# Gate products as one 512-column and one 256-column matmul, and more vector time per product for the RWKV chain, in a hybrid gated layer on one core

## Chip, cores and metric

One core of one Trainium2 chip. The metric is the device time of one execution in microseconds. Engines are named as the profile names them: PE (TensorE matmul), PEld (its weight loads), DVE (VectorE), ACT (ScalarE), POOL (GpSimd, which also issues the chain's DMAs), SP (SyncE, which issues the weight loads). Line numbers are those of the kernel before; the changed kernel's are one higher.

## What is computed

One layer for 256 tokens of width 2048. A normed input is projected to four gate sections (2048 columns each) and to four mixers of width 512: a gated linear recurrence (branch a), forgetting attention ("Fox", branch b), an SSD branch (c) and an RWKV-7 branch (d). The part that the change touches is

```
gates = sigmoid(xn @ w_gate).reshape(B, S, 4, D)
merged = sum over j of gates[:, :, j] * (branch_j @ w_branch[j])
h = h + merged @ w_out
```

and the RWKV-7 branch, a recurrence over tokens with a 64x64 state in each of 8 heads. A gated feed-forward (`w_up`, a 3-tap convolution, `w_down`) and a second gated input follow.

## The kernel before

**Products in three parts.** Activations lie transposed, in 16 row blocks of 128 by 256 tokens. A value is split into a high part and a remainder, and a product is hi·hi + hi·lo + lo·hi. Weights come from DRAM in chunks of 512 KB (`chunk`, L205, four buffers `wr`). ACT makes the high part `wh` (L214) and VectorE the remainder `wl` (L215), in three buffers each. An activation block `x` holds its high part in columns 0 to 255 and its remainder in columns 256 to 511.

`gemm_fm` takes four chunks to a block of two 128-row halves. Given such an `x`, it calls `product`: `wh` against all 512 columns of `x`, `wl` against the first 256. The result has two parts, and `joined` brings them together (an ACT copy, L256, and a VectorE addition). Given a pair of tiles, it issues three matmuls of 256 columns into one 256-column result. The gates take the pair form (`xg`, the halves of `xs`), and their evacuation is one VectorE multiplication by the row scale `R` straight from PSUM, then a tanh on ACT. All of these matmuls have the line L132 and write tiles `pg`.

**Order of the work.** After the projections come 32 gate blocks, eight to a branch, in the order a, c, b (Fox), d (RWKV). In the first three branches each gate block is followed by a branch block (`branch_unit`: 24 matmuls with the split branch output, from tiles `sb`). The gates of d are done alone, and its branch blocks at the end. Before the first block of a branch, `ready` splits the branch's four output tiles into eight tiles of the pool `bp` (36 buffers), which the RWKV chain uses too.

**The RWKV chain.** It is a generator, launched after the last projection. `hook` calls `pump` after each half of each chunk. A pump adds RATE to a credit, of at most three times RATE. If the credit is positive, it lets the generator run to its next `yield` and subtracts the vector time that the step recorded, a fixed STEP, and RATE times the number that the `yield` hands over (a pause in pumps). The chain's instructions have a lower priority than the gates' on every engine but TensorE, where they are put 16 places behind the current product. A list scheduler in the build sets the final order of each engine from these priorities and from what is ready by its own time.

The chain has these parts: token shift; per-head quantities for four blocks j, which end in masked 64x64 products (tiles `beb`, `kab`) and go to DRAM as `rw_j`; a loop of 31 steps on VectorE that inverts 32x32 triangles (a product and a reduction, L930); a copy of the inverse on ACT (L935); two writes to DRAM (`rw_q`, L937 and L938); six loads of it back as blocks (`qbd`, L945, and `qat`, L941); two blocks of small matmuls, first `qat` x `ltb`, copied to `xt1` by L952, then `qbd` x `xt1`; four steps over 64 tokens each, c = 0 to 3, with transposes (copies L1002), products with `qbd`, and a state update; and a per-head normalization. Its matmuls have the line L135 and write tiles `pb`. Only after all this can the branch blocks of d begin.

Of the kernel before, what the change touches and what calls it, by code (L numbers as in the profile page):

```python
# [11 lines left out]
ALU = mybir.AluOpType  # L12
# [3 lines left out]
S = 256  # L16
# [3 lines left out]

DELAY, RATE, STEP = 16, 0.5, 0.2
D_FF = 5632
NF = D_FF // P
IN_COLS = 14092
# [59 lines left out]
def body(tc, T, out, dbg=None):  # L86
# [5 lines left out]
    def shape_n(ap):  # L92
        n = 1
        for s in ap.shape[1:]:
            n *= s
        return n

    def tt(o, a, b, op):
        cost[0] += 0.07 + shape_n(o) / 960.0
        V.tensor_tensor(o, a, b, op=op)  # L100

    def mul(o, a, b):
        tt(o, a, b, ALU.mult)

    def add(o, a, b):
        tt(o, a, b, ALU.add)
# [19 lines left out]
    def act(o, i, f, **kw):  # L126
        A.activation(o, i, f, **kw)  # L127
# [10 lines left out]
    def mm(o, l, r, start=True, stop=True):  # L138
        on_pe(PE.matmul, o, l, r, start=start, stop=stop)
# [11 lines left out]
    def lane(name):  # L151
        prio[cur[0]] = tc.cur_priority
        cur[0] = name
        tc.cur_priority = prio[name]
# [13 lines left out]
    def slot(dt=F32, pool=sp):  # L168
        return pool.tile([P, S], dt, name="sb" if pool is not sp else "s", tag="s")

    def bank():
        return psB.tile([P, 512], F32, name="pb", tag="pb")
# [9 lines left out]
    def bslot(dt=F32):  # L182
        return slot(dt, bp)
# [19 lines left out]
    def chunk(src, kn, cols, eng=None):  # L203
        wr = wp.tile([P, kn, cols], F32, name="wr", tag="wr", bufs=4)
        (eng or dma_w).dma_start(wr, src)  # L205
        return wr
# [3 lines left out]
    def split(wr, kn, cols):  # L210

        wh = wp.tile([P, kn, cols], F32R, name="wh", tag="wh", bufs=3)
        wl = wp.tile([P, kn, cols], F32R, name="wl", tag="wl", bufs=3)
        A.copy(wh, wr)  # L214
        V.tensor_tensor(wl, wr, wh.bitcast(F32), op=ALU.subtract)  # L215
        newest[0] = wl
        return [(wh[:, i], wl[:, i]) for i in range(kn)]
# [21 lines left out]
    def halves(x):  # L239
        return (x[:, :S], x[:, S:]) if not isinstance(x, tuple) else x  # L240

    def product(pt, xs, k, nk, ms, w, fresh=True):


        wh, wl = w
        x = xs[k]
        if k == 0:
            mm(pt, wh[:, ms], x, start=fresh, stop=False)
            mm(pt[:, :S], wl[:, ms], x[:, :S], start=False, stop=False)
        else:  # L250
            mm(pt[:, :S], wl[:, ms], x[:, :S], start=False, stop=False)
            mm(pt, wh[:, ms], x, start=False, stop=k == nk - 1)

    def joined(o, pt):

        A.copy(o, pt[:, S:])  # L256
        add(o, o, pt[:, :S])

    def gemm_fm(W, xs, evac, each=None):

        ncol = S if each is None else 2 * S
        nm, nk = ncol // P, KD if each else len(xs)
        pts = [(gbank if m < 2 else bank)() for m in range(nm)]
        step = 1024 // ncol
        k0 = 0
        if each is not None:
            lane("m")
            for i in range(3):  # L270
                mm(pts[0], warm[:, :P], warm, start=i == 0, stop=False)
        while k0 < nk:
            kn = min(step, nk - k0)
            lane("g")
            if each is not None:
                kn = 1 if k0 < 4 else 2
            if each is None:
                w = chunk(W[k0 // step].rearrange("p (k n) -> p k n", k=kn), kn, ncol)
            else:
                w = chunk(W[k0:k0 + kn].rearrange("k p n -> p k n"), kn, ncol)  # L280
                each(k0, kn)
            w = split(w, kn, ncol)
            lane("m")
            for m in range(nm):
                ms = slice(m * P, m * P + P)
                for k in range(kn):
                    if not isinstance(xs[k0 + k], tuple):
                        product(pts[m], xs, k0 + k, nk, ms, w[k], not (each and m == 0))
                        continue
                    xh, xl = xs[k0 + k]  # L290
                    wh, wl = w[k]
                    first, last = k0 + k == 0, k0 + k == nk - 1
                    pt = pts[m][:, :S]
                    mm(pt, wh[:, ms], xh, start=first, stop=False)
                    mm(pt, wh[:, ms], xl, start=False, stop=False)
                    mm(pt, wl[:, ms], xh, start=False, stop=last)
                if hook[0]:
                    hook[0]()
            k0 += kn
        lane("g")  # L300
        if each is not None:
            each(nk, 0)
        for m in range(nm):
            evac(m, pts[m])
        lane("b")
# [25 lines left out]
    def mm2(o, l, src, start=True, stop=True, pool=sp):  # L331

        h, lo = split_act(src, pool=pool)
        mm(o, l, h, start=start, stop=False)
        mm(o, l, lo, start=False, stop=stop)
# [34 lines left out]
    xraw, xs = [], []  # L370
# [19 lines left out]
    R = cst.tile([P, S], F32, name="R")  # L390
# [415 lines left out]
    def rwkv():  # L806
# [3 lines left out]
        u = raw["du"]  # L810
# [10 lines left out]
        pt = bank()  # L821
        for j in range(4):
            s = bslot()
# [119 lines left out]
        for hb in range(4):  # L943
            bs = slice(hb * 32, hb * 32 + 32)
            dq.dma_start(qbd[bs, :, (hb % 2) * 32:(hb % 2) * 32 + 32],  # L945
                         bass.AP(tensor=q_d.tensor, offset=q_d.offset + hb * 16 * 1024, ap=blk))
        yield 9
        px = bank()
        for i in range(16):
            for h in (1, 0):  # L950
# [14 lines left out]
        for c in range(4):  # L965
# [27 lines left out]
            for k in (3, 2, 1, 0):  # L993
                if k not in tk and k + 1 not in tk:
                    continue
                pt = bank()
# [34 lines left out]
        for j in range(4):  # L1031
            pt = bank()
            mm2(pt[:, :S], center, yT[:, j], pool=bp)
            o = bslot()
            A.copy(o, pt[:, :S])
            yc.append(o)
            yield
        for j in range(4):
            s = bslot()
            act(s, yc[j], AF.Square)  # L1040
            mm2(pr[:8, :S], selR[:, j], s, j == 0, j == 3, bp)
            yield
        w = [bslot() for _ in range(3)]
        rstd_of(w[0][:8], pr[:8, :S], 64.0, 64e-5, w[1][:8], w[2][:8])
        nbc = head_bcast(bcast_rows(w[0][:8], 8, "rw_gn"))
# [41 lines left out]

    active = []

    credit = [0.0]  # L1090

    def pump():

        credit[0] = min(credit[0] + RATE, 3 * RATE)
        if not active or credit[0] <= 0:
            return
        was = cur[0]
        lane("b")
        cost[0] = STEP
        g = active[0]  # L1100
        try:
            credit[0] -= RATE * (next(g) or 0)
        except StopIteration:
            active.remove(g)
        credit[0] -= cost[0]
        lane(was)
# [7 lines left out]
    def proj(name, u0, n):  # L1114
        raw[name] = []
        for u in range(n):
            gemm_fm(T["w_p"][u0 + u], xs, evac_raw(raw[name]))
# [3 lines left out]
    def launch(name, f):  # L1121
        gens[name] = f()
        active.append(gens[name])
# [28 lines left out]
    launch("b", fox)  # L1152
    proj("du", 12, 7)
    launch("d", rwkv)


    merged = [None] * KD
# [1 line left out]
    order = [(0, "a"), (2, "c"), (1, "b"), (3, "d")]  # L1159
    gates = {}  # L1160

    xg = [halves(x) for x in xs]

    def gate_unit(j, u, pool):
        def ev_g(m, pt):
            s = slot(pool=pool)
            tt(s, pt[:, :S], R, ALU.mult)
            act(s, s, AF.Tanh, scale=0.5)
            gates[2 * u + m] = s
        gemm_fm(T["w_g"][8 * j + u], xg, ev_g)  # L1170

    def branch_unit(j, u, first, last):
        def ev_z(m, pt):
# [22 lines left out]
    for n, (j, nm) in enumerate(order):  # L1196
        if n < 3:
            ready(j, nm)
        for u in range(8):
            gate_unit(j, u, sp if n < 3 else bp)  # L1200
            if n < 3:
                branch_unit(j, u, n == 0, False)
# [78 lines left out]
    for k in range(2):  # L1281
        s = slot()
# [17 lines left out]
    for u in range(8):  # L1300
# [9 lines left out]
        for m in range(2):  # L1310
            lane("m")
            pt = bank()
# [75 lines left out]
```

## Time and profile before

| | |
|---|---|
| median of 3 runs | 1732.07 us (1731.74 to 1732.73) |
| profiled execution | 1731.33 us, of it span 1729.4 us |
| PE / PEld busy | 99% / 90% |
| DVE / ACT / POOL busy | 71% / 55% / 5% |
| mean DMA rate | 196 GB/s |
| granted TensorE clock, mean | 0.999 |

Shares are busy time over the span. In the window rows, an engine's name is followed by its busy time in that stretch and, in brackets, its number of instructions; PEclk is the granted clock, and the two last numbers are the DMA engines' share and GB/s. In the chain of waits a piece is its start, its length and its work. In a group, "x48 | 19.6, 416" is the count, the busy time in us and the mean of one in ns.

### The profile page before, as it was taken

Reading aid. Unit: us, or ns where it says so; the run is one execution under the profiler, and the core shown is the slowest. Engines: PE = TensorE matmul, PEld = TensorE weight load, DVE = VectorE, ACT = ScalarE, POOL = GpSimd, SP = SyncE. Lnnn points to the kernel's source line nnn. Section 1 sums busy time; section 2 is a strip of 40 time slices with the busy share of each in tenths; the row PEclk is TensorE's granted clock in tenths of the full one; section 3 lists DMA queues with packets and bytes.
Section 4 is the critical chain, followed back from the end, with each engine's and each line's share of the span. In section 5 each row is a group of like instructions: output and inputs, shape, how many; then the busy total and the mean of one; then the engine's idle time right before and its main releaser. Section 6 shows DMA issues by size and latency. Waiting matters only on the chain.

```text
span 1729.4 us, 29615 instructions
## 1 busy us (share of the span) xinstructions
PE 1713.1 (99%) x11555; PEld 1558.2 (90%) x11555; DVE 1235.8 (71%) x2006; ACT 946.1 (55%) x1426; POOL 92.6 (5%) x155
## 2 busy tenths in 40 slices
PE   8999999999999999999999999999999999999998
PEld 7888888999999999999888888888888888888887
DVE  6888768687789744648778777777777755555676
ACT  6676555556644444545556555555555544444454
POOL 1000000002320100000210000000000000000000
PEclk9999999999999999999999999999999999999999
DMA  9556556556775854665766666666656666666564
GB/s 330 172 170 217 170 175 225 184 179 206 207 213 178 256 159 150 180 185 189 249 209 192 186 193 187 191 189 189 192 188 202 211 208 189 195 193 186 179 217 139
DMA packets 99132, 338.36 MB, mean 196 GB/s; under 512 B 12362, under 2 KB 16624, under 8 KB 98736
## 3 DMA queue, kind: packets, MB, share of 16 engines
q1 hardware_dynamic: 90528, 310.94, 57.6%
q0 software_dynamic: 7456, 21.81, 4.3%
q10 hardware_dynamic: 1008, 3.73, 0.5%
q8 instruction: 90, 1.47, 0.3%
q14 instruction: 50, 0.41, 0.1%
HBM read 326.95 MB, written 9.48 MB: 195 GB/s over the span
## 4 chain that ended last, share of the span: by engine, by line
PE 94%; DVE 2%; DMA 2%; issue 1%; ACT 1%; SPq 0%; DVEq 0%; ACTq 0%
PE pg L132 90%; PE pb L135 4%; DVE wl L215 1%; PE pb L132 1%; DMA wr<-in_w_p_dram 1%; DMA cbr<-in_consts_dram 0%; DVE e L100 0%; DMA d<-in_xT_dram 0%; ACT wh L214 0%; DVE e L930 0%; DMA wr<-in_w_ax_dram 0%; DVE s L100 0%; ACT e L127 0%; DVE sb L100 0%; DVE s L120 0%
## 5 line engine op out<-in xcount | busy, mean ns | idle before, releaser
L132 PE MATMUL pg<-x,wh 128*128 128x512 f32 (+1 forms) x4384 | 1170.9, 339 | 5.5 <-DVE sb L100 5.3
L215 DVE TENSOR_TENSOR wl<-wr,wh 128x1024 fp32r<-128x1024 f32 (+1 forms) x592 | 715.5, 1210 | 408.1 <-ACT wh L214 400.5
L214 ACT CAST wh<-wr 128x1024 fp32r<-128x1024 f32 (+1 forms) x592 | 615.7, 1041 | 648.0 <-PE pg L132 495.9
L132 PE MATMUL pg<-x,wl 128*128 128x256 f32 (+1 forms) x3344 | 918.3, 282 | 3.4 <-DVE wl L215 3.4
L132 PEld LDWEIGHTS pg<-x,wh 128*128 128x128 f32 x4384 | 746.7, 188 | 91.2 <-DVE sb L100 3.1
L132 PEld LDWEIGHTS pg<-x,wl 128*128 128x128 f32 (+1 forms) x3344 | 628.8, 188 | 17.4 <-DVE wl L215 5.4
L132 PE MATMUL pg<-f,wh 128*128 128x512 f32 x704 | 243.2, 390 | 0.0
L132 PE MATMUL pg<-f,wl 128*128 128x256 f32 x704 | 195.8, 282 | 0.0
L132 PEld LDWEIGHTS pg<-f,wh 128*128 128x128 f32 x704 | 131.7, 188 | 26.9
L132 PEld LDWEIGHTS pg<-f,wl 128*128 128x128 f32 x704 | 133.0, 189 | 1.0
L132 PE MATMUL pg<-sb,wh 128*128 128x256 f32 x512 | 94.7, 283 | 0.0
L120 DVE SCALAR_TENSOR_TENSOR s<-s,prm 128x255 f32<-128x255 f32 (+1 forms) x176 | 84.1, 478 | 1.7 <-ACT s L127 1.0
L132 PEld LDWEIGHTS pg<-sb,wh 128*128 128x128 f32 x512 | 79.2, 188 | 0.1
L256 ACT COPY s<-pg 128x256 f32<-128x256 f32 x136 | 49.7, 366 | 45.8 <-PE pg L132 45.8
L132 PE MATMUL pg<-sb,wl 128*128 128x256 f32 x256 | 72.5, 284 | 0.0
L100 DVE TENSOR_TENSOR s<-s 128x256 f32<-128x256 f32 (+1 forms) x172 | 70.5, 419 | 1.6 <-ACT s L127 0.4
L127 ACT ACTIVATE s<-s 128x256 f32<-128x256 f32 x140 | 56.6, 413 | 14.9 <-DVE s L100 14.5
L100 DVE TENSOR_TENSOR s<-s,pg 128x256 f32<-128x256 f32 x136 | 56.1, 414 | 8.3 <-ACT s L256 6.6
L127 ACT ACTIVATE s<-s,prm 128x256 f32<-128x256 f32 x88 | 52.4, 596 | 0.7 <-DVE s L100 0.7
L127 ACT ACT_TABLE_LOAD x38 | 48.8, 1283 | 1.8 <-PEq L1378 1.2
L132 PEld LDWEIGHTS pg<-sb,wl 128*128 128x128 f32 x256 | 48.0, 188 | 0.2
L132 PE MATMUL pg<-d,wh 128*128 128x512 f32 x128 | 45.2, 395 | 0.0
(235 smaller groups left out, 1152.3 us busy)
## 6 DMA issues: line engine op xcount, KB each, us to landing
wr<-in_w_up_dram SPq DMA_DIRECT2D x176, 512.0 KB, 4.2
wr<-in_w_g_dram SPq DMA_DIRECT2D x128, 512.0 KB, 3.6
wr<-in_w_down_dram SPq DMA_DIRECT2D x88, 512.0 KB, 4.0
wr<-in_w_p_dram SPq DMA_DIRECT2D x76, 512.0 KB, 3.7
wr<-in_w_branch_dram SPq DMA_DIRECT2D x32, 512.0 KB, 3.7
wr<-in_w_out_dram SPq DMA_DIRECT2D x32, 512.0 KB, 3.8
wr<-in_w_ple_gate_dram SPq DMA_DIRECT2D x32, 512.0 KB, 4.2
wr<-in_w_v_dram SPq DMA_DIRECT2D x8, 512.0 KB, 4.4
```

Source lines behind the costliest of these rows:

```text
L100: V.tensor_tensor(o, a, b, op=op)
L120: V.scalar_tensor_tensor(o, a, s, b, op0=op0, op1=op1)
L127: A.activation(o, i, f, **kw)
L132: return f(*a, **kw)
L135: f(*a, **kw)
L214: A.copy(wh, wr)
L215: V.tensor_tensor(wl, wr, wh.bitcast(F32), op=ALU.subtract)
L256: A.copy(o, pt[:, S:])
```

## The change

The gates take the two-product form, with the longer evacuation. From the launch of the RWKV chain on, the credit of a pump is 0.7 in place of 0.5. The pause before the `qat` products is 5 pumps in place of 9. In the normalization, the steps of the four centred tiles and of their squares are no longer separated by a `yield` each: there is one behind each loop.

```diff
-DELAY, RATE, STEP = 16, 0.5, 0.2
+DELAY, RATE, RATE_D, STEP = 16, 0.5, 0.7, 0.2
...
-        yield 9
+        yield 5
...
             yc.append(o)
-            yield
+        yield
...
             mm2(pr[:8, :S], selR[:, j], s, j == 0, j == 3, bp)
-            yield
+        yield
...
-    credit = [0.0]
+    credit, rate = [0.0], [RATE]
...
-        credit[0] = min(credit[0] + RATE, 3 * RATE)
+        credit[0] = min(credit[0] + rate[0], 3 * rate[0])
...
-            credit[0] -= RATE * (next(g) or 0)
+            credit[0] -= rate[0] * (next(g) or 0)
...
     launch("d", rwkv)
+    rate[0] = RATE_D
...
-    xg = [halves(x) for x in xs]
-
     def gate_unit(j, u, pool):
         def ev_g(m, pt):
             s = slot(pool=pool)
-            tt(s, pt[:, :S], R, ALU.mult)
+            joined(s, pt)
+            mul(s, s, R)
             act(s, s, AF.Tanh, scale=0.5)
             gates[2 * u + m] = s
-        gemm_fm(T["w_g"][8 * j + u], xg, ev_g)
+        gemm_fm(T["w_g"][8 * j + u], xs, ev_g)
```

Three places show what the scheduler makes of it.

TensorE, at the chain's first product on the inverse (`qat` x `ltb`). Before, in the fourth chunk of the 21st gate block:

```order
L132 MATMUL pg_6883<-x_307,wh_7046 128x256 x2
L132 MATMUL pg_6883<-x_307,wl_7047 128x256
L132 MATMUL pg_6883<-x_310,wh_7046 128x256
L135 MATMUL pb_6963<-qat_408,ltb_406 64x32
L132 MATMUL pg_6883<-x_310,wh_7046 128x256
L135 MATMUL pb_6963<-qat_408,ltb_406 64x32 x31
L132 MATMUL pg_6883<-x_310,wl_7047 128x256
L132 MATMUL pg_6883<-x_336,wh_7046 128x256 x2
```

Now, behind the fourth chunk of the 17th gate block, which is the first of Fox; pg_6171 is the result of Fox's first branch block:

```order
L133 MATMUL pg_5958<-x_339,wl_6128 128x256
L133 MATMUL pg_5958<-x_339,wh_6127 128x512
L136 MATMUL pb_5623<-qat_408,ltb_406 64x32 x32
L136 MATMUL pb_5677<-qbd_410,xt1_412 64x32 x32
L136 MATMUL pb_5726<-cbr_381,e_5721 64x128 x4
L136 MATMUL pb_5746<-cbr_381,e_5721 128x128 x4
...
L136 MATMUL pb_6008<-sb_5875,e_5907 64x64 x2
L136 MATMUL pb_6008<-sb_5911,e_5907 64x64 x2
L133 MATMUL pg_6171<-sb_5941,wh_6175 128x256
L133 MATMUL pg_6171<-sb_5942,wh_6175 128x256
```

The product has moved four gate blocks forward, and from it to pg_6171 there are 160 matmuls of the chain with none of the gates or branches among them.

ACT, at the copy of the inverse (L935 before, L936 now; the tile is the loop's). Before:

```order
L214 CAST wh_6675<-wr_6673 128x1024
L214 CAST wh_6711<-wr_6709 128x1024
L935 COPY e_5554<-e_5553 64x32x32
L214 CAST wh_6743<-wr_6741 128x1024
L127 ACTIVATE s_6665<-s_6665 128x256
L127 ACTIVATE s_6668<-s_6668 128x256
```

Now; pg_5957 and pg_5958 are the two halves of the 17th gate block:

```order
L215 CAST wh_6236<-wr_6234 128x1024
L257 COPY s_6161<-pg_5957 128x256
L257 COPY s_6166<-pg_5958 128x256
L215 CAST wh_6315<-wr_6313 128x1024
L936 COPY e_4746<-e_4745 64x32x32
L128 ACTIVATE s_6161<-s_6161 128x256
L128 ACTIVATE s_6166<-s_6166 128x256
L953 COPY xt1_412<-pb_5623 128x16x32
```

The copy stands behind the evacuation copies of the block behind which TensorE has the `qat` product.

TensorE, at the chain's masked products for one j (tiles `beb`, `kab`), near the first SSD branch block. Before, for j = 0:

```order
L132 MATMUL pg_4527<-sb_2989,wl_4531 128x256
L135 MATMUL pb_4624<-d_4546,beb_402 128x128
L132 MATMUL pg_4592<-x_119,wh_4596 128x256 x2
L135 MATMUL pb_4480<-sb_4482,exc_387 128x256
L132 MATMUL pg_4592<-x_119,wl_4597 128x256
L132 MATMUL pg_4592<-x_137,wh_4596 128x256 x2
```

Now, for j = 2, behind the fourth chunk of the 9th gate block; pg_4672 is the result of the first SSD branch block:

```order
L133 MATMUL pg_4525<-x_339,wh_4633 128x512
L136 MATMUL pb_4388<-sb_4389,exc_387 128x256
L136 MATMUL pb_4474<-d_4420,beb_402 128x128 x2
L136 MATMUL pb_4475<-d_4420,kab_404 128x128
L136 MATMUL pb_4474<-d_4420,beb_402 128x128
...
L136 MATMUL pb_4540<-sb_3654,e_3458 128x256 x2
L136 MATMUL pb_4388<-sb_4390,exc_387 128x256
L136 MATMUL pb_4547<-sb_3665,d_3459 128x256
L133 MATMUL pg_4672<-sb_4508,wh_4676 128x256
```

The chain's products here stood among those of the gates and now stand in a row of 13 between a gate block and a branch block.

## Prediction

> **What bounds the kernel now.** I read the page first: span, busy times, chain.
>
> ```profile
> span 1729.4 us, 29615 instructions
> PE 1713.1 (99%) x11555; PEld 1558.2 (90%) x11555; DVE 1235.8 (71%) x2006; ACT 946.1 (55%) x1426; POOL 92.6 (5%) x155
> PE 94%; DVE 2%; DMA 2%; issue 1%; ACT 1%; SPq 0%; DVEq 0%; ACTq 0%
> ```
>
> TensorE is busy for 99% of the span and carries 94% of the chain: any time in which it stands still is added to the end. Second I cut the stretch that the change touches, from the first gate block's weights (276 us) to the last branch products (785 us), into windows.
>
> ```profile
> core 0: us, PE busy (x) PEld busy (x) DVE busy (x) ACT busy (x) POOL busy (x), PEclk, DMA share, GB/s
> 276.00:490.00 214.00, 213.83 (x1750) 210.33 (x1749) 161.42 (x300) 127.45 (x204) 37.65 (x56) 1.00 0.66 203
> 490.00:566.00 76.00, 76.00 (x645) 75.97 (x643) 70.88 (x114) 31.18 (x37) 4.87 (x8) 1.00 0.65 188
> 566.00:710.00 144.00, 140.91 (x1570) 136.49 (x1569) 79.52 (x111) 69.80 (x111) 9.19 (x14) 0.99 0.59 186
> 710.00:785.00 75.00, 75.00 (x634) 75.00 (x633) 44.72 (x64) 34.16 (x48) 4.08 (x7) 0.99 0.62 188
> ```
>
> TensorE idles 3.3 us of 509 here, although the RWKV chain with its waits runs inside this stretch. So the chain costs TensorE its own products and nothing else, because they come late enough. VectorE is at 93% from 490 to 566 us, where the chain's 31-step loop runs: no room there, much of it elsewhere.
>
> **The gate products.** Two rows give the price of the two forms: the first, from the chain of waits, is pure three-product work; the second, a window, is w_out, w_up and w_down, which already use the two-product form.
>
> ```profile
> 485.95 50.43 PE pg L132 x427
> 899.59:1632.00 732.41, 732.41 (x4221) 647.51 (x4221) 511.71 (x775) 395.28 (x582) 9.70 (x18) 1.00 0.63 193
> ```
>
> 50.43 / 427 = 118.1 ns a matmul, 354.3 ns for three. 732.41 / 4221 = 173.5 ns, 347.0 ns for two. There are 32 gate blocks x 16 rows x 2 halves = 1024 such triples: 1024 x 7.2 ns = **-7.4 us**, bounds -5 and -8.
>
> The Trainium skill (TensorE: Matmul & The Clock Gate, Back-to-back issue gap) gives about 131 ns sustained for a 512-column matmul in a stream of weight loads; by that the pair would be an estimated 249 ns and the gain about 108 us. The window's 347 ns stands against it and decides.
>
> The longer evacuation is ACT's copy and one more VectorE pass for each of 64 tiles.
>
> ```profile
> L256 ACT COPY s<-pg 128x256 f32<-128x256 f32 x136 | 49.7, 366 | 45.8 <-PE pg L132 45.8
> L100 DVE TENSOR_TENSOR s<-s,R 128x256 f32<-128x256 f32 x104 | 43.8, 422 | 1.9
> ```
>
> 64 x 0.366 = 23 us on ACT, 64 x 0.422 = 27 us on VectorE, over 509 us in which they are busy 263 and 357 us. The same evacuation in the window above leaves TensorE at 732.41 of 732.41 us, so I cost it at nothing beside TensorE; the cover is thin only where the chain crowds VectorE (last term).
>
> **The stall that goes.** Late gate evacuations held TensorE once; the window rows on both sides give the clock.
>
> ```profile
> PE pg L132 <- DVE sb L100: 2.9, 1, 2.9
> 705.32:708.19 2.87, 0.00 (x1) 0.00 (x0) 2.87 (x4) 2.82 (x4) 0.00 (x0) 0.91 0.53 174
> 708.19:711.20 3.01, 3.01 (x14) 3.01 (x15) 2.10 (x6) 2.47 (x5) 0.53 (x1) 0.51 0.58 174
> ```
>
> 2.87 us idle, then 3.0 us at half the granted clock, which loses another 1.5. In the changed order the chain is over before the last branch's gates, and no four evacuations queue: **-4.4 us**, bounds -4.4 and 0.
>
> **The wait that comes.** The chain is moved about four gate blocks forward: its first product on the inverse (qat x ltb) stood inside the 21st gate block and now stands behind the last product of the 17th. What it waits for did not move as far. In the changed ACT order the copy of the inverse (L936, formerly L935) stands behind both evacuations of that same 17th block and one weight cast, and only then can the DRAM round trip start that the product waits for. Call the end of the block's last product T. How the trip ran before, by engine and by the issue table:
>
> ```profile
> 577.96 1.15 DVE L930 TENSOR_REDUCE e<-e 64x31 f32<-64x961 f32 x1
> 579.18 2.14 ACT L935 COPY e<-e 64x1024 f32<-64x1024 f32 x1 [2.99 <-DVE e L930]
> ```
>
> ```profile
> 581.61 0.55 POOL L937 DMA_DIRECT2D rw_q<-e  x1 [1.39 <-ACT e L935]
> 586.30 2.64 POOL L945 DMA_DIRECT2D qbd<-rw_q  x4 [4.14 <-DMA rw_q<-e]
> 589.04 1.29 POOL L941 DMA_DIRECT2D qat<-rw_q  x2
> ```
>
> ```profile
> 603.86 0.30 PE L135 MATMUL pb<-qat,ltb 64*64 64x32 f32 x2
> 585.00:591.00 6.00, 6.00 (x54) 6.00 (x53) 3.46 (x4) 3.16 (x3) 4.32 (x7) 1.00 1.03 328
> h_dram<-s POOLq DMA_DIRECT2D x16, 128.0 KB, 3.2
> d<-rw_gn POOLq DMA_DIRECT2D x4, 128.0 KB, 3.1
> qat<-rw_q POOLq DMA_DIRECT2D x2, 64.0 KB, 7.3
> L214 ACT CAST wh<-wr 128x1024 fp32r<-128x1024 f32 (+1 forms) x592 | 615.7, 1041 | 648.0 <-PE pg L132 495.9
> ```
>
> Before, the copy ended at 581.32, the last load was issued at about 589.7 and landed 7.3 us later, at 597.0: 15.7 us, and TensorE came for it at 603.9, so the trip was hidden with 7 us to spare. Now ACT needs 0.37 + 1.05 + 2.14 = 3.6 us from T to the copy's end. Behind that come 0.3 us to the write, the write, 3.3 us of issues, and the loads. With the measured 4.7 and 7.3 us (DMA engines at share 1.03) that is 15.7; with the quickest like rows, 3.2 and 3.1 us, it is 9.9. Weight loads stop once four buffers are full, so I take the write as measured and the loads at 5 us, between the two: 13.3. TensorE has nothing else in its order: **+16.9 us**, bounds 13.5 and 19.3. All that stands behind it, the Fox branch's products and the remaining gates, waits.
>
> The Trainium skill (DMA: Bandwidth & Descriptors, Anatomy of one DMA) puts a transfer on this path at about 2.0 us plus its bytes over 436 GB/s. An estimate from that is 2.6 us for the write and 2.2 for the loads, a wait of about 12.1 us and a sum near 1741. The 4.7 and 7.3 us of this trace are far over it, so I stay with the rows.
>
> **The chain with nothing beside it.** Behind that product the changed TensorE order has 160 chain products in one run (inverse, first 64-token step, half of the second) before the Fox branch's first product, which itself waits for a cast that ACT does behind the first step's copies. Chain of waits, tiles and groups of before:
>
> ```profile
> 604.47 1.98 PE pb L135 x62
> 609.58 2.54 PE pb L135 x68
> 622.94 0.61 PE pb L135 x16
> 626.46 2.06 PE pb L135 x64
> 636.38 1.75 PE pb L135 x16
> L952 ACT COPY xt<-pb x1: 588/588/588, 606.5 to 606.5; 128x512 f32<-128x512 f32 x1
> L127 ACT ACTIVATE qbd<-pb x2: 589/590/591, 611.6 to 612.2; 32x512 f32<-32x512 f32 x2
> L1002 ACT COPY sb<-pb 64x256 f32<-64x256 f32 x20 | 7.3, 367 | 4.7 <-PE pb L135 4.2
> ```
>
> TensorE's own work, paid before too: 2.2 and 2.1 for the two blocks, 32 transposes at 0.11 = 3.5, and 0.6 + 0.6 + 2.1 + 1.2 for the step: 12.3 us. The path through ACT: 0.6 + 1.2 + six copies at 0.37 + two evacuations at 0.37 + 0.6 + three copies + one cast = 6.8, between them 5.4 of products behind the first block's 2.2, and some ten hand-overs of an estimated 0.1: 15.4 us. Idle **+3.1 us**, bounds 0 and 6. The wait is longer than the 2.87 us that halved the clock: one waking **+1.5 us**, bounds 0 and 4 (the run's short waits may keep it low).
>
> **Crowded VectorE.** At the end of the gate block ahead of the SSD branch's first product the new TensorE order has 13 chain products in a row, the first of them behind both evacuations, a weight cast, its own cast and four block copies on ACT.
>
> ```profile
> L221 ACT CAST sb<-sb 128x256 fp32r<-128x256 f32 x38 | 14.5, 403 | 6.0 <-DVE sb L120 4.3 <-DVE sb L100 1.4
> L896 ACT COPY kab<-d 64x256 f32<-64x256 f32 x8 | 3.2, 405 | 0.2
> ```
>
> 0.37 + 1.05 + 0.40 + 4 x 0.405 = 3.4 us less 0.1 of work between: 3.3 idle. For the loop, with more vector time a product and thus VectorE above the 93% of before, I add 0.7. **+4.0 us**, bounds 1 and 8.
>
> **Sum**, on the profiled execution's 1731.33 us: -7.4 - 4.4 + 16.9 + 3.1 + 1.5 + 4.0 = +13.7, so 1745.0. The median of the runs, 1732.07, is 0.7 above that execution: **1746**.
>
> **Rivals.**
> Heavier: the trip as slow as before (19.3), idle 6, clock 4, crowding 8: -11.8 + 37.3 gives 1757. For it: VectorE's 93%. Against: the loads run beside fewer weights.
> Lighter: trip 13.5, no idle in the run, full clock, crowding 1: -11.8 + 14.5 gives 1735. For it: 3.1-us loads exist. Against: even they start 3.6 us after T.
> Not slower: the 512-column matmul is much cheaper in the gates than I read it. Place: the 1024 pairs. It decides from a saving of 21.1 / 1024 = 20.6 ns a triple, where it pays the waits; at the 118.1 ns of a 256-column one it would save 121 us and give 1633. The sustained figure of the Trainium skill above is this case. Against it: 347.0 ns over 4221 matmuls of the same shapes.
> That the pauses do not shorten is excluded by the order.
>
> **How the numbers follow.** Forecast 0.78, with 1739 to 1753 as its own range by the bounds; heavier 0.12, lighter 0.06, not slower 0.04. The range reaches half into the heavier case: 1738 to 1755. A difference of 0.2% (3.5 us) is what a measurement can tell here. Slower 0.95, within 0.2% 0.01, faster 0.04.
>
> **What would show it.** Right: TensorE idle for 14 to 19 us in one piece before the first product on qat, POOL's write of the inverse issued after that gate block, granted clock near 0.5 behind it, no VectorE stall near 705 us, and pure gate work at 347 ns a pair. Wrong: qat loaded before TensorE reaches it, the idle time spread over many places instead, or gate pairs far from 347 ns.

## The result, and the profile after

The changed kernel takes 1759.43 us (median of 4 runs, 1757.82 to 1760.39) beside 1732.4 for the kernel before: a ratio of 1.0158, 95% interval 1.0146 to 1.0171, so 27 us slower. The forecast was 1746 with a range of 1738 to 1755. The direction and the place of the largest wait were right, the size was not: the result lies beyond the heavier rival too.

The head of the page after, its engines and its chain of waits:

```profile
span 1755.9 us, 27654 instructions
PE 1716.1 (98%) x10531; PEld 1516.1 (86%) x10531; DVE 1257.6 (72%) x2070; ACT 965.7 (55%) x1490; POOL 92.8 (5%) x155
PE 84%; issue 8%; DVE 3%; DMA 3%; ACT 1%; POOL 0%; SPq 0%; DVEq 0%; POOLq 0%; ACTq 0%
```

TensorE has 1024 matmuls less and is busy 3 us more. It carries 84% of the chain and not 94%: between 350 and 690 us much of the chain lies off TensorE, on VectorE, on the RWKV chain's DMAs, and in "issue", time in which the profile shows nothing that was waited for. TensorE's largest waits in the whole run:

```profile
PE pb L136 <- DMA qat<-rw_q: 14.2, 1, 14.2
PE pg L133 <- DVE s L101: 7.1, 3, 4.6
PE pg L133 <- DVE wl L216: 3.4, 5, 2.5
PE pg L133 <- DVE sb L101: 2.4, 2, 1.5
PE pb L136 <- ACT sb L222: 2.4, 1, 2.4
PE pg L133 <- DVE e L374: 1.5, 1, 1.5
PE pb L136 <- ACT beb L897: 1.2, 1, 1.2
PE pb L136 <- ACT xt L953: 0.7, 1, 0.7
```

The second row was 0.2 us before and was not in the forecast. Windows around the waits show what each also does to the granted clock (last column but two):

```profile
398.45:403.02 4.57, 0.00 (x2) 0.00 (x1) 2.73 (x6) 0.41 (x1) 0.00 (x0) 0.94 0.42 99
403.02:406.00 2.98, 2.98 (x10) 2.59 (x11) 2.98 (x8) 2.22 (x5) 2.24 (x3) 0.52 0.74 230
440.30:443.00 2.70, 2.70 (x12) 2.70 (x13) 0.71 (x3) 2.67 (x7) 0.01 (x1) 0.50 0.87 238
574.63:578.30 3.67, 3.67 (x64) 3.58 (x64) 0.00 (x0) 0.00 (x0) 0.00 (x0) 0.50 0.78 279
579.02:586.10 7.08, 7.08 (x80) 6.60 (x80) 0.00 (x0) 2.98 (x7) 0.00 (x0) 0.50 0.00 0
684.17:686.31 2.14, 0.01 (x1) 0.00 (x0) 2.14 (x5) 0.98 (x1) 0.00 (x0) 1.00 0.21 56
686.31:689.37 3.06, 3.05 (x16) 2.44 (x16) 3.06 (x7) 0.76 (x2) 0.00 (x0) 1.00 0.47 174
```

Half clock lasts 3 us where gates follow the wait (403, 440 us), but 12 us where the chain's small products follow it (574 to 586 us).

From 276 to 930 us TensorE is busy 650.74 us before and 626.95 us after: 3.26 and 27.05 us idle. The half clock loses (busy time times one minus the clock, in windows of 2 us) 1.5 and 8.5 us. That is +23.8 and +7.0; the profiled runs differ by 1757.82 - 1731.33 = 26.5, so 4.3 us were gained elsewhere, in the products.

Where VectorE stood at 398 us (three rows of its timeline; others lie between them), and the end of the inverse as VectorE, ACT, POOL and TensorE show it:

```profile
394.22 0.42 DVE L101 TENSOR_TENSOR sb<-sb 128x256 f32<-128x256 f32 x1
400.29 0.48 DVE L121 SCALAR_TENSOR_TENSOR sb<-sb,stamp,d 128x256 f32<-128x256 f32 x1 [5.64 <-DMA d<-rw_kn]
402.55 0.41 DVE L101 TENSOR_TENSOR s<-s,pg 128x256 f32<-128x256 f32 x1
```

```profile
560.97 1.14 DVE L931 TENSOR_REDUCE e<-e 64x31 f32<-64x961 f32 x1
562.18 1.99 ACT L936 COPY e<-e 64x1024 f32<-64x1024 f32 x1 [0.39 <-issue]
564.46 0.54 POOL L938 DMA_DIRECT2D rw_q<-e  x1 [1.24 <-ACT e L936]
569.04 2.64 POOL L946 DMA_DIRECT2D qbd<-rw_q  x4 [4.03 <-DMA rw_q<-e]
571.67 1.29 POOL L942 DMA_DIRECT2D qat<-rw_q  x2
574.63 3.71 PE L136 MATMUL pb<-qat,ltb 64*64 64x32 f32 x64 [14.20 <-DMA qat<-rw_q]
```

In the first, a chain step waits 5.64 us in VectorE's queue for a load; the gate evacuation that frees TensorE's bank (`s<-s,pg`) is the fourth instruction behind it. In the second, TensorE was done with the 17th gate block at 560.43 (574.63 - 14.20), but VectorE ended the inverse only at 562.11.

### The profile page after: what moved, and what is told of

Read it like the earlier page. It is cut to its first block, busy times and chain, and to the rows that moved or that the text cites. A ratio compares the mean times of both kernels' runs of the same rounds, so it can differ in the third digit from the quotient of the medians.

```text
span 1755.9 us, 27654 instructions
## 1 busy us (share of the span) xinstructions
PE 1716.1 (98%) x10531; PEld 1516.1 (86%) x10531; DVE 1257.6 (72%) x2070; ACT 965.7 (55%) x1490; POOL 92.8 (5%) x155
## 4 chain that ended last, share of the span: by engine, by line
PE 84%; issue 8%; DVE 3%; DMA 3%; ACT 1%; POOL 0%; SPq 0%; DVEq 0%; POOLq 0%; ACTq 0%
PE pg L133 81%; PE pb L136 2%; DVE wl L216 1%; PE pb L133 1%; DVE e L101 1%; DMA wr<-in_w_p_dram 0%; DVE s L101 0%; DVE sb L121 0%; DMA cbr<-in_consts_dram 0%; DMA d<-in_xT_dram 0%; DMA d<-rw_kn 0%; DMA rw_q<-e 0%; DVE e L931 0%; DMA d<-rw_gn 0%; ACT wh L215 0%
## 5 line engine op out<-in xcount | busy, mean ns | idle before, releaser
L216 DVE TENSOR_TENSOR wl<-wr,wh 128x1024 fp32r<-128x1024 f32 (+1 forms) x592 | 715.5, 1209 | 389.0 <-ACT wh L215 382.7
L133 PEld LDWEIGHTS pg<-x,wh 128*128 128x128 f32 (+1 forms) x3360 | 622.8, 187 | 130.6 <-DVE s L101 7.7
L133 PEld LDWEIGHTS pg<-f,wh 128*128 128x128 f32 x704 | 131.7, 188 | 26.9
L257 ACT COPY s<-pg 128x256 f32<-128x256 f32 x184 | 67.3, 367 | 71.2 <-PE pg L133 71.2
L101 DVE TENSOR_TENSOR s<-s,pg 128x256 f32<-128x256 f32 x184 | 75.4, 413 | 7.8 <-ACT s L257 6.0
L101 DVE TENSOR_TENSOR s<-s,R 128x256 f32<-128x256 f32 x152 | 63.5, 420 | 2.5
```

Of the source, the lines that this page charges most:

```text
L133: return f(*a, **kw)
```

## The experiments

The theory after reading the trace was that the pacing had moved the chain ahead of what VectorE and the DRAM trip could deliver, while the gate form gained its 5 us; the first rival, that the longer evacuation was the loss. Edits are against the changed kernel unless said otherwise. Each group was timed beside the kernel before (1731.7 to 1733.0).

**One half of the change at a time.** gates_alone keeps only the gate products and their evacuation:

```diff
-DELAY, RATE, RATE_D, STEP = 16, 0.5, 0.7, 0.2
+DELAY, RATE, RATE_D, STEP = 16, 0.5, 0.5, 0.2
...
-        yield 5
+        yield 9
         px = bank()
...
             yc.append(o)
-        yield
+            yield
...
             mm2(pr[:8, :S], selR[:, j], s, j == 0, j == 3, bp)
-        yield
+            yield
```

> The changed gate products and their longer evacuation, with the chain's rate, pause and yields as before. Theory A (the pacing is the loss, the gate form a small gain): a gate row costs 347.5 ns in place of 352.6, 1024 x 5.1 ns = 5.2 us, and no wait on qat comes: 1727 us, 1725 to 1730. Theory B (the longer evacuation is the loss: PSUM banks held by ACT's copy and a VectorE addition that queues behind the chain): stalls of several us behind VectorE remain with the old pacing too: 1736 us or more.

1741.35 us, ratio 1.0053 (1.0038 to 1.0068). Theory A failed: the gate form alone loses, as B's number said. pacing_alone is the other half:

```diff
+    xg = [halves(x) for x in xs]
...
-            joined(s, pt)
-            mul(s, s, R)
+            tt(s, pt[:, :S], R, ALU.mult)
...
-        gemm_fm(T["w_g"][8 * j + u], xs, ev_g)
+        gemm_fm(T["w_g"][8 * j + u], xg, ev_g)
```

> Rate 0.7, the pause of 5 and the joined loops, with the three-product gates of before. Theory A: the product on qat stands behind the 17th gate block here too, so the trip's wait of about 14 us, the half clock behind it (about 5 us) and VectorE's waits for chain loads are all here, without the 5.2 us of gain: 1760 us, 1755 to 1765. Theory B: ACT's copy of the inverse is not behind evacuations now and VectorE has one pass less a tile: 1745 us or less.

1735.25 us, ratio 1.0028 (1.0017 to 1.0039). So the halves cost 9 and 4 us, and together 27: most of the loss is in their meeting. The product on qat waits 1.7 us in the traced execution, though it stands behind the same gate block:

```profile
532.94 1.16 DVE L931 TENSOR_REDUCE e<-e 64x31 f32<-64x961 f32 x1
552.26 2.79 PE L136 MATMUL pb<-qat,ltb 64*64 64x32 f32 x64 [1.75 <-DMA qat<-rw_q]
```

The inverse is done at 534.1 us, 16 us before TensorE wants it, in place of 1.7 us after. Two more undo one number of the pacing each, pause9 (`yield 5` to `yield 9`) and rate05 (`RATE_D` 0.7 to 0.5):

> The changed kernel with the pause of 9 restored. Theory A1 (the rate of 0.7 sets the place of the product on qat): the order has it behind the 17th block as with 5, with ACT's copy at the same place, so the same wait of 14 us; only the run of chain products behind it is shorter (96 in place of 160): 1755 us, 1752 to 1759. Theory A2 (the shorter pause is the cause): four pumps of about 1.7 us come back, 7 us of wait and some of the half clock: 1748 us or less.

1759.7 us, ratio 1.0156 (1.0139 to 1.0173), wait on qat 14.5 us. The pause of 5 or 9 makes no difference: the scheduler puts the product behind the 17th block either way (A1, 0.7 us over its range).

> The changed kernel with the rate of 0.5, so gate form, pause of 5 and joined loops stay. Theory A1: the product on qat is back in the 21st gate block region and the trip is hidden: like the gate form alone, 1727 us, 1725 to 1731. Theory A2 (the pause is the cause): about 7 us of wait and half a clock behind it remain: 1737 us or more.

1746.86 us, ratio 1.0089 (1.0074 to 1.0104). The wait on qat is gone, so the rate sets its place; but stalls of 3.6 and 4.4 us at 713 to 735 us came in. A1's number failed.

**Products or evacuation.** form_old and form_new keep the two-product form but evacuate as before, which leaves hi·lo out of the gates; pool_new and pool_old do the whole evacuation, with the multiplication by R on GpSimd. The pairs differ in the pacing (old: as before; new: as changed). The first edit is that of form_old and form_new, the second that of pool_old and pool_new.

```diff
-            joined(s, pt)
-            mul(s, s, R)
+            tt(s, pt[:, :S], R, ALU.mult)
```

```diff
             joined(s, pt)
-            mul(s, s, R)
+            G.tensor_tensor(s, s, R, op=ALU.mult)
```

> The two-product gates with the evacuation of before (the second result column block is left unread, so the gates lack hi x lo), and the chain's pacing of before. Theory C (the loss of the gate form is the second VectorE pass and the ACT copy of its evacuation, not the products): the stalls behind VectorE go, 5 us of products are gained: 1727 us, 1724 to 1729. Theory D (faster rows of products leave VectorE less time per weight chunk, whatever the evacuation): 1736 us or more, stalls remain.

1735.86 us, ratio 1.0016 (1.0007 to 1.0026).

> The same products and evacuation with the changed pacing. Theory C: in VectorE's order the inverse loop ends three weight splits ahead of the 17th block's evacuation, as with the pacing alone, so the wait on qat falls from 14 us to under 4: like the pacing alone less 5, 1730 us, 1727 to 1734. Theory D: the loop still ends too late, 1748 us or more.

1748.78 us, ratio 1.0085 (1.0070 to 1.0100); wait on qat 10.1 us in the traced execution, which took 1744.8. This is theory D's number.

> The changed kernel with the multiplication by R of the gate evacuation on GpSimd in place of VectorE; everything is computed. Theory C: VectorE has one pass a tile as before, the loop ends about four splits earlier than in the changed kernel, the wait on qat is under 4 us and the 4.6 us hold behind VectorE goes: 1733 us, 1728 to 1738. Theory E (GpSimd's pass is slow, is in the way of VectorE or holds up the chain's DMA issues behind it): 1745 us or more.

1750.66 us, ratio 1.0099 (1.0084 to 1.0114); wait on qat 7.8 us.

> The gate form alone (pacing of before) with the multiplication by R on GpSimd. Theory C: 1728 us, 1725 to 1731, a version that beats both. Theory E: 1738 us or more.

1742.78 us, ratio 1.0055 (1.0040 to 1.0070).

Theory C failed in its numbers: without the longer evacuation the gate form still loses. Against the full evacuation (gates_alone, the changed kernel) it costs 5.5 and 10.7 us less (6.4 and 12.6 by the ratios, because the kernel before took 1733.0 in this group), so the evacuation is part of the loss, not all. GpSimd was no way out: its multiplication takes 1064 ns a tile where VectorE's takes 0.42 us (48 tiles of pool_old; 988 ns in pool_new). Waits for weight remainders rise from 3.4 us to 8.2 (pool_new), but pause17 below has 7.5 us of them without GpSimd's help, so that rise is not shown to be GpSimd's.

**The chain's waits.** pause17 makes the qat pause 17; kn12 makes the pause behind the row norms' load (`rw_kn`) 12 in place of 6; all_pauses does both and makes the last one (`rw_gn`) 12.

```diff
         nbc = head_bcast(bcast_rows(w[0][:8], 8, "rw_kn"))
-        yield 6
+        yield 12
...
-        yield 5
+        yield 17
         px = bank()
...
         nbc = head_bcast(bcast_rows(w[0][:8], 8, "rw_gn"))
-        yield 6
+        yield 12
```

> The changed kernel with a pause of 17 before the qat products in place of 5: in the order they stand two gate blocks later (28 us), and the run of 160 is split. Theory F (in the changed kernel the wait costs 14.2 us idle, 1.6 us of short waits in the run behind it and about 5.7 us of half clock, and all of it hangs on this place): 21 us less, 1738 us, 1734 to 1742. Theory F2 (the chain's later end meets the last gates, and the loss comes back there): 1746 us or more.

1744.97 us, ratio 1.0077 (1.0062 to 1.0092). No wait on qat and full clock there, as F said; of its 21 us, 14 are kept, and new stalls of 3.2 and 1.5 us, with half clock between them, end at 715.7 and 724.6 us (F2 in part).

> The changed kernel with a pause of 12 pumps in place of 6 behind the row norms' trip through DRAM. Theory I (the 4.6 us idle and 1.5 us half clock at 398 us come from VectorE standing in its queue for that load): these 6 us go, and with the run of 13 gone from the order at the next chain part also some of its 3.6 and 1.4 us: 1750 us, 1746 to 1753. Theory J (the evacuations queue behind the chain in any case): 1756 us or more.

1759.4 us, ratio 1.0160 (1.0144 to 1.0175): no gain. Theory I failed, and how it failed tells most. TensorE's stalls at 398 and 440 us shrank from 8.2 to 3.4 us, and the wait on qat grew by 5.8:

```profile
402.67 0.50 PE L133 MATMUL pg<-x,wh 128*128 128x512 f32 x1 [3.39 <-DVE s L101]
574.61 1.67 PE L136 MATMUL pb<-qat,ltb 64*64 64x32 f32 x26 [20.03 <-DMA qat<-rw_q]
```

The product starts at 574.61 us, in the changed kernel at 574.63. Up to there the chain on VectorE sets the time, and a stall of TensorE ahead of it costs nothing.

> Pauses of 12, 17 and 12 (row norms, qat, group norm) in the changed kernel. If theories F and I hold and the two add: 1730 us, 1724 to 1736, near or below the kernel before. If the waits come back in other places: 1742 us or more.

1743.96 us, ratio 1.0072 (1.0057 to 1.0087). A wait of 11.3 us has appeared at the chain's end.

**The clock.** fill puts 34 dense products into the wait on qat:

```diff
+        dm = bslot(F32R)[:, :P]
+        A.copy(dm, xs[2][:, :P])
+        A.copy(dm[:64], prod.rearrange("p a b -> p (a b)")[:, :P])
         px = bank()
+        for i in range(34):
+            mm(px, dm, xs[i % 16])
```

> The changed kernel with 34 products of 128x128 by 512 columns added in front of the qat product, into its PSUM bank, which it overwrites; they wait for ACT's copy of the inverse, so they lie in the last 10 us of the wait. Theory G (the clock is lowered by the wait, and the small products behind it do not raise it, dense ones do within 3 us): the run behind the wait goes at full clock, its first 64 records take 2.0 us in place of 3.7, 5.7 us less: 1753 us, 1751 to 1755. Theory H (the small products of the chain keep the clock low whatever was before): no gain, 1758 us or more.

1758.12 us, ratio 1.0158 (1.0141 to 1.0175). Its windows (dense products to 576.3, small ones from there):

```profile
565.81:569.00 3.19, 3.19 (x8) 2.51 (x9) 1.15 (x3) 0.75 (x2) 0.45 (x1) 0.50 0.95 335
572.00:576.30 4.30, 4.30 (x19) 3.20 (x17) 0.00 (x0) 0.00 (x0) 2.99 (x5) 1.00 0.48 110
576.33:579.00 2.67, 2.06 (x65) 1.94 (x64) 0.00 (x0) 0.57 (x1) 0.00 (x0) 1.00 0.89 348
579.00:581.50 2.50, 2.43 (x68) 2.37 (x69) 0.00 (x0) 0.35 (x2) 0.00 (x0) 0.98 0.06 18
581.50:585.00 3.50, 3.50 (x30) 3.17 (x28) 0.00 (x0) 3.04 (x8) 0.00 (x0) 0.53 0.02 5
```

G and H each hold in part: dense work raises the clock and the first 64 records take 2.06 us and not 3.7, but after 5 us of small products alone the clock falls again, with TensorE busy. The added products end at 576.3 us, 1.7 us behind the point where the changed kernel's chain went on. The median is 1.3 us lower and the ratio the same, so no gain is clear of the noise. The traced execution of pacing_alone shows a fall behind a wait of 1.75 us only:

```profile
550.50:552.20 1.70, 0.01 (x1) 0.00 (x0) 0.96 (x1) 0.70 (x1) 0.00 (x0) 1.00 1.00 371
556.00:560.00 4.00, 4.00 (x42) 3.78 (x41) 1.36 (x3) 1.78 (x3) 0.00 (x0) 0.50 0.15 58
560.00:564.00 4.00, 4.00 (x50) 3.83 (x49) 0.71 (x1) 1.56 (x4) 0.00 (x0) 0.50 0.40 135
```

Behind that wait TensorE did the 64 products on qat, then 3.5 us of gate products (555.0 to 558.5 us), then the chain's next products, and the clock was at half for 13.7 us. This does not happen each time. In the traced execution and two more of the ten, the mean granted clock was 0.995 to 0.996 and the time 1740 to 1741 us; in the other seven it was 0.998 or 0.999 and the time 1734 to 1736 us, which leaves room for about 7 us at half (2 x 0.002 x 1735) and not for 13.7. So the chain's small products can lower the clock, or keep it low, when they stand alone or behind a short wait; how many it takes is not settled. Before, the same products stood between gates at a clock of 1.00:

```profile
603.00:640.00 37.00, 37.00 (x466) 35.49 (x466) 16.18 (x22) 18.18 (x32) 0.75 (x1) 1.00 0.53 171
```

**A rate between.** With the gate form, the old pause and the old yields, g055 and g06 set the rate to 0.55 and 0.6. o055 has the old gates and 0.55, f055 the gate form with the old evacuation (hi·lo left out) and 0.55.

```diff
-DELAY, RATE, RATE_D, STEP = 16, 0.5, 0.7, 0.2
+DELAY, RATE, RATE_D, STEP = 16, 0.5, 0.55, 0.2
...
-        yield 5
+        yield 9
         px = bank()
```

> The gate form with a rate of 0.55, pause of 9 and yields of before. In the order TensorE takes 194 weight chunks before the qat product and VectorE ends the inverse after 188 (changed kernel: 180 and 181; gate form alone: 200 and 194), and the chain's last products are spread again (gate form alone: 11 in one run behind the last gate but one). Theory K (the products gain 5 us, and what was lost hung on these two places): no wait on qat, no run at 705 us: 1730 us, 1727 to 1733. Theory L (the gate form costs VectorE and evacuation waits wherever the chain stands): 1738 us or more.

1746.87 us, ratio 1.0081 (1.0068 to 1.0094).

> The same with a rate of 0.6 (193 chunks against 187; runs of 11, 13 and 11 chain products near 400 us come back). Theory K: no wait on qat, but a few us at 400 us: 1733 us, 1729 to 1737. Theory L: 1738 us or more.

1744.73 us, ratio 1.0067 (1.0051 to 1.0082).

> The three-product gates of before with a rate of 0.55, all else as before (192 chunks against 186; the chain ends six tiles earlier than in the kernel before). The stall at 705 us of 2.9 us and 1.5 us of half clock goes: 1728 us, 1726 to 1732. If the stall only moves: 1731 us or more. Against g055 it gives the gate form's worth: theory K -5 to +2 us for g055, theory L +6 or more.

1733.82 us, ratio 1.0005 (0.9995 to 1.0014). The stall at 705 us is gone, and yet no gain is clear of the noise: the executions spread from 1729 to 1737 us.

> As g055, with the gates' evacuation of before (the second result column block is left unread, so hi x lo is missing): the two-product form without a second VectorE pass. Theory K: 1726 us, 1723 to 1730, 3 to 5 us under g055 at most. Theory M (the products alone cost time at this pacing too): 1733 us or more.

1738.21 us, ratio 1.0032 (1.0020 to 1.0045). TensorE waits 11.2 us at the chain's end, up to 715.5 us.

K failed for g055 by 17 us, but the whole of it is in one place, at the chain's end, where VectorE waits for the load of the group norm and the evacuations of the fourth branch's gates stand behind it (VectorE and TensorE of g055):

```profile
716.07 0.88 DVE L121 SCALAR_TENSOR_TENSOR sb<-sb,stamp,d 128x256 f32<-128x256 f32 x2 [5.51 <-DMA d<-rw_gn]
722.15 0.75 DVE L101 TENSOR_TENSOR sb<-sb,pg 128x256 f32<-128x256 f32 x2
722.72 0.76 PE L133 MATMUL pg<-x,wh 128*128 128x512 f32 x1 [14.67 <-DVE sb L101]
```

ACT's copy of the same tiles waits too, until 721.68, although TensorE had stood still since 708.1 (722.72 - 14.67). These gates (tiles `sb`) lie in `bp`, the chain's own pool. Two last kernels take `sp` for the first three of these blocks, one at rate 0.55, one at 0.5:

```diff
-            gate_unit(j, u, sp if n < 3 else bp)
+            gate_unit(j, u, sp if n < 3 or u < 3 else bp)
```

> The kernel of g055 (gate form, rate 0.55), with the gates of the first three d blocks put in the pool sp and not in bp, where the chain's tiles lie. TensorE's order through the chain is the same; in VectorE's order the first three evacuations now stand ahead of the chain's last steps. Theory N (the 14.7 us of g055 is the d gates waiting for bp buffers that the chain holds until its last load): that wait and the 2.6 us of half clock behind it go: 1729 us, 1727 to 1733. Theory O (the evacuations queue behind VectorE's wait for the load whatever their pool): 1740 us or more.

1730.79 us, ratio 0.9993 (0.9984 to 1.0002). Theory N holds: the wait is gone, 16 us with the clock, by a change of the tiles' pool alone. Whether the tiles waited for buffers or for their place in the queues is not separated: with the other pool the build also puts their copies and evacuations ahead of VectorE's wait for the load.

> The gate form alone (pacing of before) with the same three blocks in sp. The run of 11 chain products at the end of the gates is gone from the order too. Theory N: of the 8.2 us idle and 3 us of half clock at 705 to 720 us nearly all goes: 1731 us, 1727 to 1734. Theory O: 1739 us or more.

1742.44 us, ratio 1.0060 (1.0048 to 1.0073). The number failed. The chain ends later at this rate, and a wait of the same kind (10.3 us) now stands in front of a later gate block, whose tiles are still in `bp`; no run moves that block too:

```profile
740.46 0.88 DVE L121 SCALAR_TENSOR_TENSOR sb<-sb,stamp,d 128x256 f32<-128x256 f32 x2 [6.21 <-DMA d<-rw_gn]
750.51 0.76 PE L133 MATMUL pg<-x,wh 128*128 128x512 f32 x1 [10.28 <-DVE sb L101]
```

**All runs together.** Two counts over the runs bear on the rest. The wait on qat follows from the order: take the weight chunks that TensorE uses ahead of that product, less the weight splits that VectorE does ahead of the inverse's last step.

| kernel | chunks - splits | wait on qat, us |
|---|---|---|
| before | 200 - 191 = 9 | 0 |
| gates_alone, g055, pause17 | 200 - 194, 194 - 188, 187 - 181 = 6 | 0 |
| o055, f055, pacing_alone | 192 - 186, 192 - 186, 180 - 174 = 6 | 1.1, 0.2, 1.7 |
| pool_new | 180 - 177 = 3 | 7.8 |
| form_new | 180 - 179 = 1 | 10.1 |
| after, pause9 | 180 - 181 = -1 | 14.2, 14.5 |
| kn12 | 180 - 183 = -3 | 20.0 |

Each chunk of margin under 6 costs 2.0 to 2.6 us. The rate took TensorE's place from 200 to 180. With the old gates it took the inverse from 191 to 174, but with the new products only to 179 (form_new), and with the longer evacuation as well to 181: of the 7 splits that the changed kernel is behind pacing_alone, 5 come with the two-product form itself and 2 with its evacuation. Why the build's order sets the inverse later beside the two-product form is not shown.

The gain of the products is what is left of a profiled execution without the idle time and the half-clock loss of 276 to 930 us: 1726.6 (before), 1726.2 (o055) and 1724.4 (pacing_alone) with the old gates, mean 1725.7; with the new ones 1722.2 (after) to 1725.7 (pool_old), mean of 16 kernels without fill 1723.6. So the gain of the products is an estimated 2 to 4 us; the two groups overlap, with 1724.4 the lowest of the first.

## Why the prediction was right in sign and wrong in size

In the order of its sum, on the profiled execution (+13.7 forecast, +26.5 measured):

| term | forecast | measured |
|---|---|---|
| gate products | -7.4 (-8 to -5) | -4.3 here, 2 to 4 over all kernels |
| stall at 705 us goes | -4.4 | -4.4, but 2.4 idle at 684 to 690 us |
| wait on qat | +16.9 (13.5 to 19.3) | +14.2 |
| chain run, idle | +3.1 (0 to 6) | 0.68 + 0.47 + 0.48 = +1.6 |
| waking at half clock | +1.5 (0 to 4) | +5.6 |
| crowded VectorE | +4.0 (1 to 8) | 3.6 of waits for ACT and 1.6 of clock at 440, 4.6 and 1.4 at 398, 0.6 at 550: +11.8 |

The products are the remainder of the account, so the column closes by itself (26.9, 0.4 over from rounding and window edges); the second figure in their row is from the other kernels. Two sums of the forecast's rivals were a microsecond off: the heavier one gives 1757.6 with its 0.7 us, the one at 118.1 ns a triple 1632.

**Right.** The product on qat stands in one piece of 14.2 us behind the 17th block, and the copy of the inverse ended 3.7 us after that block (forecast 3.6). Write, issues and loads then took 10.5 us (forecast 13.3, bounds 9.9 and 15.7). The DMA issues from 560 to 576 us, with KB each and the time to landing:

```profile
rw_q<-e POOLq DMA_DIRECT2D x2, 256.0 KB, 6.2
qat<-rw_q POOLq DMA_DIRECT2D x2, 64.0 KB, 2.2
```

The loads were quicker than the quickest like row of before. The Trainium skill (DMA: Bandwidth & Descriptors, Anatomy of one DMA) gave an estimate of 2.2 us for the loads and 2.6 for the write; the first agrees with this trace, the second does not.

The part of 13 products waited 3.6 us for ACT (forecast 3.3).

**Why it waited, only half seen.** The forecast put the copy's lateness down to ACT's queue. VectorE ended the inverse 1.7 us after the block as well, 0.3 us after ACT was free. form_new and pool_new, where ACT's copy is not behind those evacuations, still wait 10.1 and 7.8 us. So the agreement of 3.7 with 3.6 us is in part luck: the two engines came free within 0.3 us of each other. The margin in splits was there to be counted in the order, and was not.

**Wrong: "one waking +1.5".** The clock was costed as a fixed 3 us at half behind a wait, from a row in which dense gates followed. Here 160 small products followed, and it stayed at half for 12 us: 5.6, over the bound of 4.

**Wrong: "I cost it at nothing beside TensorE".** The longer evacuation was priced on w_out, w_up and w_down, where no chain runs. Taking it away is worth 5.5, 8.7 and 10.7 us (gates_alone to form_old, g055 to f055, after to form_new). The sum also has no term for what the two-product form costs by its effect on the order: with the old evacuation it is still 2.9 us over the kernel before (form_old), 4.4 over o055 (f055), and 10 us or more over pacing_alone (form_new).

**Wrong: the crowding term.** It counted ACT in front of one part and 0.7 us for the loop. The 4.6 us at 398 us, VectorE standing in its queue for a load with gate evacuations behind it, are a kind of wait that the forecast saw for TensorE's queue only. In the changed kernel, though, it is hidden: kn12 shows that what is saved there is waited for at qat.

**Mis-sized: "1024 x 7.2 ns".** In stretches without chain products a pair costs 347.5 ns (700 to 780 us after) beside 352.6 for three (712 to 780 us before), 5.1 and not 7.2: the stretch from 485.95 us was taken as pure gate work, but it holds branch triples, at 0.36 us each. (Both rates here are less those triples: 65.24 us for 185 and 76.28 for 219.5.) Over the whole stretch even 5.2 us are not seen; where the other 1 to 3 us go is open. The sustained 131 ns of the Trainium skill (TensorE: Matmul & The Clock Gate, Back-to-back issue gap) stays far off: the 512-column product takes 0.23 us here.

A sum of terms was also the wrong form for this stretch: with VectorE's chain the later one up to 574.6 us, TensorE's own terms ahead of it do not add to its end.

## What to carry to other kernels

Where a slow dependent chain is threaded through a stream that keeps TensorE full, count for each hand-over how many of the stream's steps each engine has ahead of it in its own order: that margin, not the sum of busy times, tells whether the wait shows. A cheaper form of the stream shifts all these margins, so chain and stream have to be paced anew together, and only then is the gain to be seen (an estimated 2 to 4 us here, against waits of 10 to 20). A wait at the head of VectorE's queue (4.6 us at 398 us), or a buffer pool shared with the chain (14.7 us in g055), stops the stream as surely as a missing operand.

## What the runs showed of the hardware that was not expected

- TensorE's granted clock fell to half while it was busy: about 5 us into a run of the chain's small products with nothing else (fill, 581.5 us), and behind an idle of 1.75 us (pacing_alone, by the mean clock in three of ten executions). In the changed kernel it came back after 12 us of such products, in pacing_alone after 14 us of which 3.5 were gate products, in fill after 3.5; where dense products alone followed, in 3 us. The Trainium skill (TensorE: Matmul & The Clock Gate, Part 1: The HAM clock gate) says that about 3.4 us of sustained work bring the full clock, and that an idle window of 3.4 us takes it away; the trace agrees on the first where dense products alone followed (403 and 440 us).
- The length of an idle does not decide alone. An idle of 2.14 us (changed kernel, 684 us) and of 2.77 us (pool_new, 680 us) left the clock at 1.00; 2.87 us (before, 705 us) lowered it, less than the 3.4 us that the Trainium skill gives for an idle window. In all twenty traces the clock changes at steps of 3.41 us (half lasted 3.4 us in before, 13.7 in pacing_alone, 23.9 in the changed kernel from within the wait on). Among the steps at full clock, TensorE was idle for at most 1.83 us where full clock followed and for at least 1.88 us where half followed. Four falls at 0.7 to 1.75 us of idle are the exceptions (fill, o055, rate05, pacing_alone); in all four the chain's products filled part of the step. Of the three idles above, at most 1.6, 1.8 and 2.4 us lie in one step.
- A multiplication of 128x256 on GpSimd takes 1064 ns beside a busy VectorE (pool_old), and VectorE's own 2006 instructions take longer there: 1247.0 us, beside 1237.5 in form_old, which has the same count; its weight remainders take 1232 ns beside 1223.
